# Projections with extra columns instead of carries, a GpSimd copy at the end of a solve, and a state written in place (hybrid mLSTM / RWKV-7 block, one core)

## The chip, the cores and the metric

One Trainium2 chip, one of its cores. The metric is the device time of one execution in microseconds. Engines by the profile's names: PE is TensorE (PEld its weight loads), DVE is VectorE, ACT is ScalarE, POOL is GpSimd, SP is SyncE, whose queue issues all DMAs of this kernel.

## The reference, cut to what matters

One layer on 2048 tokens of width 1024: a mixer with two groups of heads (mLSTM and RWKV-7), then cross-attention, a SwiGLU FFN and a final norm. The change lies in the mixer alone. What of it matters here:

```
z = u @ w_in                                # both groups
# RWKV-7: every projected channel is mixed with the one of the token before
z = z + (token_shift(z) - z) * mu           # r, k, v, and the three low-rank inputs
# mLSTM: a causal convolution over 4 tokens, then silu
out = zp[:, 0:T] * w[0] ... + zp[:, 3:3 + T] * w[3]     # zp: 3 zeros ahead
# RWKV-7 recurrence, a 64 x 64 state S per head
sa = einsum('bhij,bhj->bhi', S, a_t)
S = S * w_t + sa * b_t + v_t * k_t ;  y_t = S r_t
```

## The kernel before, in words

Everything is computed with channels on partitions and tokens in columns. The normed input `u` lies in DRAM as two float16 parts (`u_d[0]` high, `u_d[1]` low); a product of full accuracy is three float16 matmuls (`mm3`, lines 53 to 55).

`mixer_pass` runs twice (`hq` 0 and 1), each time over half of the heads. A pass walks over 8 groups (`sg`) of 256 tokens. For each group it does:

- `load_u` (line 624): 8 DMAs bring the 256 columns of `u`.
- `prepare` for two blocks of 128 channels (`e` 0 and 1): `project` gives k, r and v of RWKV-7 in PSUM (24 matmuls of 256 columns each). `shifted` (lines 284 to 290) mixes neighbouring tokens: ACT writes `ps * mu` into columns 1 to 256 of a tile `tmu` (line 287), POOL puts the last column of the group before into column 0 (line 286) and saves the last one (line 288), and DVE adds `ps * (1 - mu)` to the shifted tile (line 289). The rest of `prepare` builds the operands of the chunk form: chunks of 64 tokens, a triangular 64 x 64 matrix `MX` per head and chunk, values `VS`, `VX`, keys `KBt`.
- `solve` (lines 400 to 452) inverts the triangular matrices. Four DMAs turn 32 x 32 blocks of `MX` through DRAM into a tile `M`, one block per partition; POOL does 31 steps of two instructions each (lines 424, 426), a chain in which each waits for the one before; ACT copies the result `X` turned into `M` (line 427, 512 elements, read with a step). Then 12 DMAs on SP: `X` to `t1d` (line 430) and `M` to `td` (line 429) in DRAM, and back as `T1` (line 434) and into `MX` (line 439). PE joins the blocks with `pps` (line 444), which waits for `T1`, and `xps` (line 450), which waits for `MX`; ACT copies each result.
- `scan` (lines 454 to 493): four chunks one after the other. First ACT copies the state `st.S` into the chunk operand `VS` (line 457). Each chunk is 16 small matmuls into `ch` with two ACT copies between (lines 464, 469), then DVE adds the old state (line 475) and multiplies by the decay into `VS` of the next chunk (line 478), or, after the fourth chunk, into a tile `Sc` (line 481).
- `mlstm` for two heads: `project` for q and k (`qps`), ACT writes the scaled product into a tile `z` at columns 3 to 258 (line 543), POOL brings and saves the three columns of the group before (lines 542, 544), ACT starts the convolution with the last tap (line 547), DVE adds three taps (line 549). `vops` (line 558, by `mm3`) gives values and gate, with `u` as the weights.

The loop is written group after group, and the order on each engine is set when the kernel is built, by the framework's own estimate of when each instruction can start. Instructions of one group are so laid between those of others: the mLSTM projections of one group fill PE while POOL solves. At run time each engine goes through its list in order; an instruction that waits holds up all behind it. PSUM tiles for projections (`mm`) and for small products (`ax`) have two buffers each.

Of the kernel before, what the change touches and what calls it, by code (L numbers as in the profile page):

```python
# [7 lines left out]
F32 = mybir.dt.float32  # L8
# [235 lines left out]
def mixer_pass(c, I, hq, tp, T):  # L244

    nc, tc = c.nc, c.tc
    SGN = 256
    w_in = I["w_in"][0]
    b0, b1 = slice(0, 64), slice(64, 128)
# [13 lines left out]

    carry = tp.k.tile([P, 2, 3], F32, tag="carry", name="carry")
    nc.gpsimd.memset(carry, 0.0)
    halo = tp.k.tile([P, 2, 2, 3], F32, tag="halo", name="halo")
    nc.gpsimd.memset(halo, 0.0)
    st = Ctx()
    st.S = tp.k.tile([P, 2, 64], F32, tag="Sc", name="Sc", bufs=3)
    nc.gpsimd.memset(st.S, 0.0)  # L270
    st.Cn = []
# [3 lines left out]

    def project(ps, j, e, u):
        for k in range(KT):
            h, l = wts[j > 2][k]
            o = (2 * (j - 3 if j > 2 else j) + e) * P
            s = slice(o, o + P)  # L280
            mm3(nc, ps, (h[:, s], l[:, s]), u[k], k == 0, k == KT - 1)

    def shifted(ps, j, e, o):
        t = tp.t2.tile([P, SGN + 1], F32, tag="tmu", name="tmu")
        m = 4 * j + 2 * hq + e
        nc.gpsimd.tensor_copy(t[:, 0:1], carry[:, e, j:j + 1])
        nc.scalar.activation(t[:, 1:SGN + 1], ps, AF.Copy, scale=c.mu_s[:, m:m + 1])
        nc.gpsimd.tensor_copy(carry[:, e, j:j + 1], t[:, SGN:SGN + 1])
        nc.vector.scalar_tensor_tensor(o, ps, c.mu_c[:, m:m + 1], t[:, 0:SGN], op0=ALU.mult, op1=ALU.add)
        return o  # L290

    def group(sg):
        G = Ctx()
        G.xwa = [tp.t2.tile([P, SGN], F16, tag=f"xwa{i}", name="xwa") for i in range(2)]
        for i in range(2):
            nc.sync.dma_start(G.xwa[i], c.l_d[0][i][:, sg * SGN:(sg + 1) * SGN])
        G.MX = tp.MX.tile([P, 2, 4, 64], F32, tag="MX", name="MX")
        G.VS = tp.sg.tile([P, 2, 4, 2, 64], F32, tag="VS", name="VS")
        G.VX = tp.sg.tile([P, 2, 4, 2, 64], F32, tag="VX", name="VX")
        G.bon = tp.sg.tile([P, 2, SGN], F32, tag="bon", name="bon")  # L300
        G.W = tp.sg.tile([P, 2, 4, 1], F32, tag="W", name="W")
        return G

    def prepare(sg, e, u, G):
# [31 lines left out]

        ps = tp.pmm.tile([P, SGN], F32, tag="mm", name="kps")
        project(ps, 1, e, u)
        k = shifted(ps, 1, e, tp.t2.tile([P, SGN], F32, tag="k", name="k"))
        ps = tp.pmm.tile([P, SGN], F32, tag="mm", name="rps")  # L340
        project(ps, 0, e, u)
        r = shifted(ps, 0, e, tp.t2.tile([P, SGN], F32, tag="r", name="r"))
        ps = tp.pmm.tile([P, SGN], F32, tag="mm", name="vps")
        project(ps, 2, e, u)
# [55 lines left out]
    def solve(MX, NG):  # L400
# [18 lines left out]
        for s in range(31):  # L419
# [6 lines left out]
            nc.gpsimd.tensor_tensor(X[:, s + 1:32, 0:ncl], X[:, s + 1:32, 0:ncl], tv, ALU.add)  # L426
        nc.scalar.copy(M[:, 0:16], X.rearrange("p r c -> p c r"))
        for e in range(2):
# [25 lines left out]
    def scan(sg, gs, G):  # L454
        y = tp.s2.tile([P, 2, 2, 2, 64], F32, tag="y", name="y")
        for h in range(2):
            nc.scalar.copy(G.VS[halves[h], :, 0, h], st.S[halves[h]])
        for n in range(4):
            ch = tp.psc.tile([P, 2, 3, 64], F32, tag="ch", name="ch")
            for e, g in enumerate(gs):  # L460
                for h in range(2):
                    nc.tensor.matmul(ch[halves[h], e, 0], lhsT=g.RR[:, n, h, 0:64], rhs=G.VS[:, e, n, h], start=True, stop=True)
            R = tp.s2.tile([P, 2, 64], F32, tag="R", name="R")
            nc.scalar.copy(R, ch[:, :, 0])
            for e, g in enumerate(gs):
                for b in halves:
                    nc.tensor.matmul(ch[b, e, 1], lhsT=g.M[b, n], rhs=R[b, e], start=True, stop=True)
            for h, b in enumerate(halves):
                nc.scalar.copy(G.VX[b, :, n, h], ch[b, :, 1])
            for e, g in enumerate(gs):  # L470
                for h in range(2):
                    last = nc.tensor.matmul(ch[halves[h], e, 2], lhsT=g.KBt[:, n, h], rhs=G.VX[:, e, n, h], start=True, stop=True)
            Sn = tp.s2.tile([P, 2, 64], F32, tag="Sn", name="Sn")
            for h, b in enumerate(halves):
                nc.vector.tensor_tensor(Sn[b], ch[b, :, 2], G.VS[b, :, n, h], ALU.add)
            if n < 3:
                for h, b in enumerate(halves):
                    nc.vector.tensor_tensor(G.VS[b, :, n + 1, h], Sn[b], G.W[b, :, n].to_broadcast([64, 2, 64]), ALU.mult)
            else:
                st.S = tp.k.tile([P, 2, 64], F32, tag="Sc", bufs=3, name="Sc")  # L480
                nc.vector.tensor_tensor(st.S, Sn, G.W[:, :, n].to_broadcast([P, 2, 64]), ALU.mult)
        yps = tp.psc.tile([P, 2, 2, 2, 64], F32, tag="Y", name="yps")
# [46 lines left out]
    def mlstm(sg, e, u):  # L529
# [8 lines left out]
        for j in range(2):  # L538
            ps = tp.pmm.tile([P, SGN], F32, tag="mm", name="qps")
            project(ps, 3 + j, e, u)  # L540
            z = m2.tile([P, SGN + 3], F32, tag="z", name="z", bufs=1)
            nc.gpsimd.tensor_copy(z[:, 0:3], halo[:, e, j])
            nc.scalar.activation(z[:, 3:SGN + 3], ps, AF.Copy, scale=DSC)
            nc.gpsimd.tensor_copy(halo[:, e, j], z[:, SGN:SGN + 3])
            a = m2.tile([P, SGN], F32, tag="cv", name="cv", bufs=1)
            cw = lambda i: col(c, R_CONV + 8 * i + 4 * j + hp)
            nc.scalar.activation(a, ps, AF.Copy, scale=c.cw3[:, 4 * j + hp:4 * j + hp + 1])  # L547
            for i in range(3):
# [10 lines left out]
        for n in range(2):  # L559
            ts = slice(n * P, (n + 1) * P)  # L560
            for k in range(KT):
                h, l = wts[1][k]
                mm3(nc, ps[:, n], (u[k][0][:, ts], u[k][1][:, ts]),
                    [x.rearrange("p (j e d) -> p j e d", j=4, e=2)[:, 2:4, e] for x in (h, l)], k == 0, k == KT - 1)
# [53 lines left out]
    def load_u(sg):  # L618
        u = []
        for k2 in range(KT // 2):  # L620
            h = tp.u.tile([P, 2, SGN], F16, tag="uh", name="uh")
            l = tp.u.tile([P, 2, SGN], F16, tag="ul", name="ul")
            for i, t in enumerate((h, l)):
                nc.sync.dma_start(t, c.u_d[i][:, 2 * k2:2 * k2 + 2, sg * SGN:(sg + 1) * SGN])
            u += [(h[:, 0], l[:, 0]), (h[:, 1], l[:, 1])]
        return u
# [8 lines left out]

    NS = T // SGN
    late = []
# [784 lines left out]
```

## Time and profile before

| | |
|---|---|
| median of 3 runs | 3060.55 us (3058.68 to 3062.34) |
| the profiled execution | 3062.21 us |
| its span, first to last instruction | 3060.5 us |
| busy in the span: PE | 2922.1 us (95%) |
| DVE, ACT, POOL | 2034.8, 1262.3, 1180.1 us |
| mean granted TensorE clock | 0.981 of 2.4 GHz |

The mixer passes lie between about 100 and 1260 us of the span; before them is the pass that norms the input, behind them output projection, attention and FFN. Busy time of PE counts each matmul to its modelled end, so a PE that is 95% busy may have little or no time to give. "Idle before" is the time in which an engine had nothing running, and the name behind the arrow is what ended it. A granted clock of 1.00 is the upper of TensorE's two levels, 0.50 the lower; a number between is a stretch that had both.

### The profile page before, as it was taken

The page shows a single profiled execution, that of the slowest core. Times are in us where ns is not written, and L with a number is a line of the kernel's source. Part 1 is how long each engine was busy: PE and PEld are TensorE (multiplying, and loading weights), DVE is VectorE, ACT ScalarE, POOL GpSimd, SP SyncE. Part 2 cuts the span into 40 slices and gives each one's busy share as a digit, 9 for nine tenths or more (in the row PEclk, how much of TensorE's full clock was granted, in tenths as well). Part 3 has the DMA queues.
Part 4 walks back from the last instruction along what each step waited for, and adds up shares of the span by engine and source line. Part 5 has one row for each costly group of instructions (what it writes and reads, how often), then busy time and mean ns, then how long its engine had stood idle before and what let it go on. Part 6 is the DMA issues. An engine that isn't in the chain of part 4 may idle for free. (4 is left out here: it accounts for less than half of the span.)

```text
span 3060.5 us, 54611 instructions
## 1 busy us (share of the span) xinstructions
PE 2922.1 (95%) x20579; PEld 1772.5 (58%) x20579; DVE 2034.8 (66%) x3652; ACT 1262.3 (41%) x2842; POOL 1180.1 (39%) x2149
## 2 busy tenths in 40 slices
PE   7899999999999988999999999999999999899998
PEld 4677877778777767665455544444444444344443
DVE  6666666777666666565588886545445555988975
ACT  6544444555444445454456653222222223423432
POOL 2164655555456654032111144222222222644542
PEclk9999999999999988999999999999999999999999
DMA  8621112232211213554223366111111121554442
GB/s 278 143 60 44 45 43 47 78 99 55 53 50 44 56 45 111 183 186 145 97 93 125 110 227 201 57 55 56 56 55 58 57 62 63 185 184 143 159 137 76
DMA packets 330212, 307.85 MB, mean 101 GB/s; under 512 B 88302, under 2 KB 280028, under 8 KB 329052
## 3 DMA queue, kind: packets, MB, share of 16 engines
q1 hardware_dynamic: 329948, 304.36, 32.3%
q8 instruction: 162, 2.65, 0.4%
q14 instruction: 102, 0.84, 0.1%
HBM read 208.79 MB, written 95.49 MB: 99 GB/s over the span
## 5 line engine op out<-in xcount | busy, mean ns | idle before, releaser
L53 PE MATMUL pp<-u,wb 128*128 128x512 f16 x1232 | 467.9, 380 | 14.0 <-DVE e L1127 9.6
L54 PE MATMUL pp<-u,wb 128*128 128x512 f16 x1232 | 467.9, 380 | 0.0
L55 PE MATMUL pp<-u,wb 128*128 128x512 f16 x1232 | 467.6, 380 | 0.0
L1127 DVE TENSOR_TENSOR e<-pp,e 128x512 f32<-128x512 f32 x308 | 208.5, 689 | 302.0 <-PE pp L55 289.1
L55 PE MATMUL dps<-w,gS 128*128 128x512 f16 x616 | 233.4, 379 | 9.0 <-DVE gS L49 9.0
L54 PE MATMUL dps<-w,gS 128*128 128x512 f16 x616 | 233.5, 379 | 1.7 <-DVE w L49 1.7
L53 PE MATMUL dps<-w,gS 128*128 128x512 f16 x616 | 233.5, 379 | 0.0
L424 POOL TENSOR_TENSOR tmp<-M,X 64x126 f32<-64x126 f32 (+22 forms) x496 | 189.1, 381 | 98.8 <-DMA M<-md 71.4
L426 POOL TENSOR_TENSOR X<-X,tmp 64x126 f32<-64x126 f32 (+22 forms) x496 | 202.2, 408 | 29.0
L54 PEld LDWEIGHTS <-wb 128*128 128x128 f16 x1232 | 120.7, 98 | 156.5 <-issue 12.9
L53 PEld LDWEIGHTS <-wb 128*128 128x128 f16 x1232 | 120.8, 98 | 151.0 <-DMA u<-u_d 5.4
L55 PEld LDWEIGHTS <-wb 128*128 128x128 f16 x1232 | 120.7, 98 | 146.3 <-issue 1.1
L1143 POOL TENSOR_TENSOR S<-raw 128x512 f32<-128x512 f32 x22 | 33.3, 1513 | 413.4 <-DVE wb L49 413.4
L53 PE MATMUL qps<-uh,wh 128*128 128x256 f16 x512 | 143.8, 281 | 9.5 <-ACT cv L547 9.5
L53 PE MATMUL vops<-wh,uh 128*128 128x256 f16 x512 | 143.2, 280 | 3.1 <-ACT cv L547 3.1
L54 PEld LDWEIGHTS <-wh 128*128 128x128 f16 x1280 | 127.1, 99 | 31.3 <-issue 11.6
L54 PE MATMUL qps<-ul,wh 128*128 128x256 f16 x512 | 143.7, 281 | 0.0
L55 PE MATMUL qps<-uh,wl 128*128 128x256 f16 x512 | 143.5, 280 | 0.0
L55 PE MATMUL vops<-wh,ul 128*128 128x256 f16 x512 | 143.0, 279 | 0.0
L54 PE MATMUL vops<-wl,uh 128*128 128x256 f16 x512 | 142.9, 279 | 0.0
L53 PEld LDWEIGHTS <-wh 128*128 128x128 f16 x1280 | 127.1, 99 | 24.5 <-issue 2.7
L55 PEld LDWEIGHTS <-wl 128*128 128x128 f16 x1280 | 127.2, 99 | 20.6 <-issue 1.9
(423 smaller groups left out, 7637.6 us busy)
## 6 DMA issues: line engine op xcount, KB each, us to landing
g_d<-e SPq DMA_DIRECT2D x88, 256.0 KB
h<-h_d SPq DMA_DIRECT2D x32, 512.0 KB
acc<-h_d SPq DMA_DIRECT2D x32, 512.0 KB
u_d<-ub SPq DMA_DIRECT2D x56, 256.0 KB
ga<-g_d SPq DMA_DIRECT2D x32, 384.0 KB
raw<-in_ffn_w_gate_dram SPq DMA_DIRECT2D x22, 512.0 KB
raw<-in_ffn_w_up_dram SPq DMA_DIRECT2D x22, 512.0 KB
rawd<-in_ffn_w_down_dram SPq DMA_DIRECT2D x22, 512.0 KB
```

The lines of the kernel that those rows point to most:

```text
L53: nc.tensor.matmul(out, lhsT=lhs[0], rhs=rhs[0], start=start, stop=False)
L54: nc.tensor.matmul(out, lhsT=lhs[0], rhs=rhs[1], start=False, stop=False)
L55: nc.tensor.matmul(out, lhsT=lhs[1], rhs=rhs[0], start=False, stop=stop)
L424: nc.gpsimd.tensor_tensor(tv, M[:, s, s + 1:32].unsqueeze(2).to_broadcast(shp), X[:, s, 0:ncl].unsqueeze(1).to_broadcast(shp), ALU.mult)
L426: nc.gpsimd.tensor_tensor(X[:, s + 1:32, 0:ncl], X[:, s + 1:32, 0:ncl], tv, ALU.add)
L1127: add = lambda o, x, y: nc.vector.tensor_tensor(o, x, y, ALU.add)
L1143: nc.gpsimd.tensor_tensor(s[0], a[1][0], a[1][1], ALU.add)
```

## The change

- No carries: `load_u` brings 260 columns, 4 of the group before and 256 of its own (for the first group POOL writes zeros into the 4). `project` computes 257 columns for k, r and v and 259 for q and k of mLSTM, so the preceding tokens are computed again. `shifted` reads the same PSUM tile at two offsets; `z` is written whole by ACT. All `carry`, `halo` and `tmu` tiles and their 320 POOL copies go.
- The last copy of a solve (`M` from `X`) is done by POOL instead of ACT.
- The state after the fourth chunk is written by DVE in two halves straight into `VS` of the next group; the `Sc` tile, its product and the two ACT copies at the start of each scan go. After the last group of a pass no state is computed.

The diff, cut to its core:

```diff
     def project(ps, j, e, u):
...
-            mm3(nc, ps, (h[:, s], l[:, s]), u[k], k == 0, k == KT - 1)
+            mm3(nc, ps, (h[:, s], l[:, s]), [x[:, SGN + 4 - ps.shape[1]:SGN + 4] for x in u[k]], k == 0, k == KT - 1)
     def shifted(ps, j, e, o):
-        t = tp.t2.tile([P, SGN + 1], F32, tag="tmu", name="tmu")
         m = 4 * j + 2 * hq + e
-        nc.gpsimd.tensor_copy(t[:, 0:1], carry[:, e, j:j + 1])
-        nc.scalar.activation(t[:, 1:SGN + 1], ps, AF.Copy, scale=c.mu_s[:, m:m + 1])
-        nc.gpsimd.tensor_copy(carry[:, e, j:j + 1], t[:, SGN:SGN + 1])
-        nc.vector.scalar_tensor_tensor(o, ps, c.mu_c[:, m:m + 1], t[:, 0:SGN], op0=ALU.mult, op1=ALU.add)
+        nc.scalar.activation(o, ps[:, 1:SGN + 1], AF.Copy, scale=c.mu_c[:, m:m + 1])
+        nc.vector.scalar_tensor_tensor(o, ps[:, 0:SGN], c.mu_s[:, m:m + 1], o, op0=ALU.mult, op1=ALU.add)
         return o
+    def values():
+        return tp.sg.tile([P, 2, 4, 2, 64], F32, tag="VS", name="VS")
     def group(sg):
         G = Ctx()
+        G.VS = st.VS
+        if sg == 0:
+            G.VS = values()
+            for h in range(2):
+                nc.gpsimd.memset(G.VS[halves[h], :, 0, h], 0.0)
...
-        nc.scalar.copy(M[:, 0:16], X.rearrange("p r c -> p c r"))
+        nc.gpsimd.tensor_copy(M[:, 0:16], X.rearrange("p r c -> p c r"))
...
     def scan(sg, gs, G):
-        for h in range(2):
-            nc.scalar.copy(G.VS[halves[h], :, 0, h], st.S[halves[h]])
+        st.VS = values() if sg < NS - 1 else None
...
+            dst = G.VS[:, :, n + 1] if n < 3 else st.VS[:, :, 0] if st.VS is not None else None
+            if dst is None:
+                break
             Sn = tp.s2.tile([P, 2, 64], F32, tag="Sn", name="Sn")
             for h, b in enumerate(halves):
                 nc.vector.tensor_tensor(Sn[b], ch[b, :, 2], G.VS[b, :, n, h], ALU.add)
-            if n < 3:
-                for h, b in enumerate(halves):
-                    nc.vector.tensor_tensor(G.VS[b, :, n + 1, h], Sn[b], G.W[b, :, n].to_broadcast([64, 2, 64]), ALU.mult)
-            else:
-                st.S = tp.k.tile([P, 2, 64], F32, tag="Sc", bufs=3, name="Sc")
-                nc.vector.tensor_tensor(st.S, Sn, G.W[:, :, n].to_broadcast([P, 2, 64]), ALU.mult)
+            for h, b in enumerate(halves):
+                nc.vector.tensor_tensor(dst[b, :, h], Sn[b], G.W[b, :, n].to_broadcast([64, 2, 64]), ALU.mult)
...
-            nc.gpsimd.tensor_copy(z[:, 0:3], halo[:, e, j])
-            nc.scalar.activation(z[:, 3:SGN + 3], ps, AF.Copy, scale=DSC)
-            nc.gpsimd.tensor_copy(halo[:, e, j], z[:, SGN:SGN + 3])
+            nc.scalar.activation(z, ps, AF.Copy, scale=DSC)
...
-            h = tp.u.tile([P, 2, SGN], F16, tag="uh", name="uh")
+            h = tp.u.tile([P, 2, SGN + 4], F16, tag="uh", name="uh")
...
+                o = 0
+                if sg == 0:
+                    nc.gpsimd.memset(t[:, :, 0:4], 0.0)
+                    o = 4
+                nc.sync.dma_start(t[:, :, o:], c.u_d[i][:, 2 * k2:2 * k2 + 2, sg * SGN - 4 + o:(sg + 1) * SGN])
```

Since the build decides the order anew, the change also moves instructions within the mixer; from the first matmuls of the attention on, all engines have the same order as before. Two places:

SP at the end of the sixth solve of the first pass, before (`T_...` is `T1`):

```order
L430 DMA t1d<-X 16x512 x2
L429 DMA td<-M 512x1x32 x2
L434 DMA T_7497<-t1d 32x8x16 x4
L439 DMA MX<-td 32x8x32 x4
L296 DMA xwa<-l_d_88 128x256
```

The same place with the change:

```order
L431 DMA t1d<-X 16x512 x2
L435 DMA T_7343<-t1d 32x8x16 x2
L430 DMA td<-M 512x1x32 x2
L435 DMA T_7343<-t1d 32x8x16 x2
L298 DMA xwa<-l_d_88 128x256
L440 DMA MX<-td 32x8x32 x4
```

The first two loads of `T1`, which wait for `t1d` to land, have moved ahead of the two stores of `M`; 14 of the 16 solves have it so, one has one load ahead, one has the old order.

ACT around the end of the same solve, before:

```order
L543 ACTIVATE z<-qps 128x256
L547 ACTIVATE cv<-qps,cw_499 128x256
L397 COPY KBt<-kbps 128x4x64
L551 ACTIVATE th<-cv 128x256
L427 COPY M<-X 64x512
L397 COPY KBt<-kbps 128x4x64
L543 ACTIVATE z<-qps 128x256
L547 ACTIVATE cv<-qps,cw_499 128x256
```

The same place with the change:

```order
L541 ACTIVATE z<-qps 128x259
L544 ACTIVATE cv<-qps,cw_499 128x256
L548 ACTIVATE th<-cv 128x256
L541 ACTIVATE z<-qps 128x259
L398 COPY KBt<-kbps 128x4x64
L544 ACTIVATE cv<-qps,cw_499 128x256
L398 COPY KBt<-kbps 128x4x64
L548 ACTIVATE th<-cv 128x256
```

The copy of `M` is gone from between the two copies of `KBt` that empty PSUM for PE; the rest stands in much the same order.

## Rows read from the trace of the kernel before

**Rows 1.** The page: busy us over the span, share, instructions.

```profile
PE 2922.1 (95%) x20579; PEld 1772.5 (58%) x20579; DVE 2034.8 (66%) x3652; ACT 1262.3 (41%) x2842; POOL 1180.1 (39%) x2149
```

**Rows 2.** Busy time by stretch: the mixer, and all behind it. Columns: start and end, length, then busy us (instructions) of PE, PEld, DVE, ACT, POOL, granted clock, DMA share, GB/s.

```profile
130.00:1200.00 1070.00, 1011.56 (x10555) 820.67 (x10552) 716.66 (x1714) 505.22 (x1431) 592.59 (x1595) 0.96 0.24 56
1262.00:3060.00 1798.00, 1755.00 (x8515) 839.03 (x8513) 1192.16 (x1665) 637.37 (x1168) 554.60 (x450) 1.00 0.34 114
```

**Rows 3.** The longest waits of PE between 180 and 1180 us: us in total, times, longest.

```profile
PE pps L444 <- DMA T<-t1d: 10.3, 12, 1.8
PE kbps L395 <- ACT KBt L397: 6.8, 7, 2.6
PE qps L53 <- ACT cv L547: 5.4, 8, 1.8
```

**Rows 4.** The timeline of PE, nine of its stops (seven behind an ACT copy, two for `T1`): start, length, instruction, and in brackets the idle time before it and what ended it.

```profile
254.96 0.81 PE L444 MATMUL pps<-T,MX 32*32 32x32 f32 x30 [1.81 <-DMA T<-t1d]
...
394.21 0.46 PE L395 MATMUL kbps<-ident,KB 64*128 64x64 f32 x4 [1.69 <-ACT KBt L397]
...
463.66 0.37 PE L53 MATMUL vops<-wh,uh 128*128 128x256 f16 x1 [2.16 <-ACT cv L547]
...
530.59 0.48 PE L321 MATMUL wps<-xwa,lwa 64*128 64x256 f16 x3 [1.46 <-ACT KBt L397]
...
600.35 0.69 PE L395 MATMUL kbps<-ident,KB 64*128 64x64 f32 x4 [2.58 <-ACT KBt L397]
...
602.02 0.79 PE L321 MATMUL wps<-xwa,lwa 64*128 64x256 f16 x3 [0.98 <-ACT KBt L397]
...
745.10 0.21 PE L444 MATMUL pps<-T,MX 32*32 32x32 f32 x2 [1.26 <-DMA T<-t1d]
...
796.77 0.33 PE L462 MATMUL ch<-VS,RR 128*64 128x64 f32 x2 [2.52 <-ACT VS L457]
...
1075.17 1.22 PE L350 MATMUL sps<-sq,bones 128*128 128x256 f32 x2 [4.09 <-ACT sq L348]
```

**Rows 5.** Busy time in the stretches of the seven ACT stops, columns as in rows 2.

```profile
392.00:402.00 10.00, 8.31 (x77) 5.95 (x76) 5.01 (x12) 5.29 (x15) 4.56 (x10) 0.83 0.32 54
460.00:470.00 10.00, 7.81 (x54) 5.36 (x53) 5.90 (x14) 5.20 (x14) 5.50 (x13) 0.83 0.28 45
528.00:538.00 10.00, 8.39 (x65) 5.64 (x65) 5.81 (x13) 4.92 (x14) 5.01 (x11) 0.83 0.31 54
598.00:610.00 12.00, 8.67 (x77) 5.87 (x78) 8.10 (x17) 7.27 (x19) 5.27 (x9) 0.72 0.42 91
795.00:805.00 10.00, 8.23 (x71) 6.17 (x72) 5.10 (x10) 6.21 (x16) 6.23 (x11) 0.66 0.27 42
1071.00:1095.00 24.00, 16.37 (x158) 11.63 (x157) 11.87 (x26) 9.99 (x25) 5.74 (x14) 0.57 0.19 40
```

**Rows 6.** The timeline of ACT ahead of the third stop, and all its waits for the end of a solve between 180 and 1180 us.

```profile
529.22 1.05 ACT L427 COPY M<-X 64x512 f32<-64x512 f32 x1 [1.31 <-POOL X L426]
530.17 0.36 ACT L397 COPY KBt<-kbps 128x256 f32<-128x256 f32 x1
...
ACT M L427 <- POOL X L426: 24.3, 15, 3.6
```

**Rows 7.** The timeline of PE in a run of projections at the upper clock: the second and the ninth matmul of a row of equal ones.

```profile
613.46 0.27 PE L54 MATMUL qps<-ul,wh 128*128 128x256 f16 x1
...
614.23 0.27 PE L55 MATMUL qps<-uh,wl 128*128 128x256 f16 x1
```

**Rows 8.** The timeline of SP's issues and of POOL at the end of the sixth solve (the last step of the solve ended at 529.18).

```profile
529.21 0.78 SPq L430 DMA_DIRECT2D t1d<-X  x2
530.29 1.23 SPq L429 DMA_DIRECT2D td<-M  x2
531.62 2.09 SPq L434 DMA_DIRECT2D T<-t1d  x4
534.03 1.78 SPq L439 DMA_DIRECT2D MX<-td  x4
...
531.37 0.52 POOL L414 MEMSET X<- 64x512 f32 x1 [2.05 <-DMA t1d<-X]
```

**Rows 9.** The small POOL copies (duration min/median/max in ns, then first and last start) and two waits between 180 and 1180 us, as in rows 3.

```profile
L542 POOL COPY z<-halo x64: 176/186/696, 104.0 to 1180.4; 128x3 f32<-128x3 f32 x64
...
ACT tmu L287 <- POOL carry L288: 27.8, 15, 3.6
POOL tmp L424 <- DMA M<-md: 65.0, 15, 8.0
```

**Rows 10.** Two POOL instructions by line, between 180 and 1262 us: count, busy us, mean ns, idle before.

```profile
L503 POOL TENSOR_TENSOR y<-y,var 128x512 f32<-128x512 f32 x15 | 15.6, 1042 | 0.1
L377 POOL COPY VX<-VS 64x256 f32<-64x256 f32 x60 | 25.2, 419 | 23.3 <-ACT VS L375 19.8 <-POOL z L542 0.9
```

**Rows 11.** Two more stops of PE, as in rows 4, and the product that makes the next chunk's state, by line, as in rows 10.

```profile
850.55 0.76 PE L462 MATMUL ch<-VS,RR 128*64 128x64 f32 x8 [0.62 <-ACT VS L457]
1185.48 0.33 PE L462 MATMUL ch<-VS,RR 128*64 128x64 f32 x2 [0.59 <-ACT VS L457]
...
L478 DVE TENSOR_TENSOR VS<-Sn,W 64x128 f32<-64x128 f32 x96 | 31.0, 322 | 2.0
```

**Rows 12.** Float32 matmuls of the mLSTM chunks over the whole span, as in rows 9; the moving operand of every second one starts 129 elements into its tile.

```profile
L585 PE MATMUL ncp<-vx,Em x128: 275/276/582, 152.4 to 1194.5; 128*128 128x129 f32 x128
```

More of the change, by code (lines that the diff above doesn't have):

```diff
@@ L247, in mixer_pass @@
     SGN = 256
+    NS = T // SGN
     w_in = I["w_in"][0]
@@ L262, in mixer_pass @@
             wts[n - 3].append((h, l))
[L264 to L267, printed above, removed]
     st = Ctx()
-    st.S = tp.k.tile([P, 2, 64], F32, tag="Sc", name="Sc", bufs=3)
-    nc.gpsimd.memset(st.S, 0.0)
+    st.VS = None
     st.Cn = []
@@ L297, in group @@
         G.MX = tp.MX.tile([P, 2, 4, 64], F32, tag="MX", name="MX")
-        G.VS = tp.sg.tile([P, 2, 4, 2, 64], F32, tag="VS", name="VS")
         G.VX = tp.sg.tile([P, 2, 4, 2, 64], F32, tag="VX", name="VX")
@@ L335, in prepare @@
         nc.gpsimd.tensor_copy(G.W[:, e], E[:, :, 64:65])
-        ps = tp.pmm.tile([P, SGN], F32, tag="mm", name="kps")
+        ps = tp.pmm.tile([P, SGN + 1], F32, tag="mm", name="kps")
         project(ps, 1, e, u)
         k = shifted(ps, 1, e, tp.t2.tile([P, SGN], F32, tag="k", name="k"))
-        ps = tp.pmm.tile([P, SGN], F32, tag="mm", name="rps")
+        ps = tp.pmm.tile([P, SGN + 1], F32, tag="mm", name="rps")
         project(ps, 0, e, u)
         r = shifted(ps, 0, e, tp.t2.tile([P, SGN], F32, tag="r", name="r"))
-        ps = tp.pmm.tile([P, SGN], F32, tag="mm", name="vps")
+        ps = tp.pmm.tile([P, SGN + 1], F32, tag="mm", name="vps")
         project(ps, 2, e, u)
@@ L538, in mlstm @@
         for j in range(2):
-            ps = tp.pmm.tile([P, SGN], F32, tag="mm", name="qps")
+            ps = tp.pmm.tile([P, SGN + 3], F32, tag="mm", name="qps")
             project(ps, 3 + j, e, u)
             z = m2.tile([P, SGN + 3], F32, tag="z", name="z", bufs=1)
-            nc.gpsimd.tensor_copy(z[:, 0:3], halo[:, e, j])
-            nc.scalar.activation(z[:, 3:SGN + 3], ps, AF.Copy, scale=DSC)
-            nc.gpsimd.tensor_copy(halo[:, e, j], z[:, SGN:SGN + 3])
+            nc.scalar.activation(z, ps, AF.Copy, scale=DSC)
             a = m2.tile([P, SGN], F32, tag="cv", name="cv", bufs=1)
             cw = lambda i: col(c, R_CONV + 8 * i + 4 * j + hp)
-            nc.scalar.activation(a, ps, AF.Copy, scale=c.cw3[:, 4 * j + hp:4 * j + hp + 1])
+            nc.scalar.activation(a, ps[:, 3:SGN + 3], AF.Copy, scale=c.cw3[:, 4 * j + hp:4 * j + hp + 1])
             for i in range(3):
@@ L559, in mlstm @@
         for n in range(2):
-            ts = slice(n * P, (n + 1) * P)
+            ts = slice(n * P + 4, (n + 1) * P + 4)
             for k in range(KT):
@@ L620, in load_u @@
         for k2 in range(KT // 2):
-            h = tp.u.tile([P, 2, SGN], F16, tag="uh", name="uh")
-            l = tp.u.tile([P, 2, SGN], F16, tag="ul", name="ul")
+            h = tp.u.tile([P, 2, SGN + 4], F16, tag="uh", name="uh")
+            l = tp.u.tile([P, 2, SGN + 4], F16, tag="ul", name="ul")
             for i, t in enumerate((h, l)):
-                nc.sync.dma_start(t, c.u_d[i][:, 2 * k2:2 * k2 + 2, sg * SGN:(sg + 1) * SGN])
+                o = 0
[3 more added lines that the diff above has]
+                nc.sync.dma_start(t[:, :, o:], c.u_d[i][:, 2 * k2:2 * k2 + 2, sg * SGN - 4 + o:(sg + 1) * SGN])
             u += [(h[:, 0], l[:, 0]), (h[:, 1], l[:, 1])]
@@ L634, in run_mlstm @@
                 mtails.pop(0)()
-    NS = T // SGN
     late = []
```

## The prediction

> **What bounds the kernel now.** I read the page's busy times first, then the busy time by stretch, then PE's waits, its timeline, and the timeline of the engine that PE waits for. PE is busy for 2922 of 3060 us [rows 1]. Behind the mixer it is busy for 1755 of 1798 us at a granted clock of 1.00 [rows 2], and there all engines keep their order, so I expect nothing from that part. In the mixer two things are to be seen: PE stands for 1070 - 1011.6 = 58 us, and its clock is 0.96 on average [rows 2], about 0.04 x 1012 = 40 us of work at the upper level lost. So some 100 us are there to be had, and the change can only win them by ending PE's stops, or lose by adding work to PE or new stops. PE's longest waits are for `T1`, for `KBt` and for the convolution's tile, the last two on ACT [rows 3].
>
> The clock falls where PE stood: in six stretches, each with a stop of 1.5 to 4.1 us [rows 4], the granted clock is 0.57 to 0.83 [rows 5]. A stop therefore costs its length and some slow matmuls behind it.
>
> **The change, part by part.**
>
> *Extra columns.* Seven equal matmuls of 256 columns take 614.23 - 613.46 = 0.77 us [rows 7], 0.110 us each, 0.43 ns per column. k, r and v are 2 passes x 8 groups x 2 blocks x 3 x 24 = 2304 matmuls with one column more, q and k of mLSTM 2 x 8 x 2 x 2 x 24 = 1536 with three more: 6912 columns, **+3.0 us**, on the path, since PE is the bound.
>
> *ACT's copy of the solved blocks leaves ACT.* This is the largest term. At 529.22 ACT had waited 1.31 us for POOL's last step of the solve, then copied for 1.05 us; only then came the `KBt` copy, at 530.17 [rows 6], and PE, which waited for that, went on at 530.59 after 1.46 us [rows 4]. With the wait and the copy gone, `KBt` could come 2.36 us earlier, more than the stop. Seven stops of rows 4 lie within some 3 us of such a copy, at six solves of sixteen. They sum to 15.5 us. In their stretches the lost clock is busy time x (1 - clock) [rows 5]: 1.4 + 1.3 + 1.4 + 2.4 + 2.8 + 7.0 = 16.4 us. Upper end of the gain: 32 us. What ACT gets back at a solve is on average 24.3 / 15 + 1.05 = 2.7 us [rows 6], as long as the stops of one solve, 15.5 / 6 = 2.6. Lower end: nothing, for the next latecomer is near. PE's waits for `T1` come at other solves than these stops, as at 254.96 and 745.10 [rows 4]; where a stop of ACT came first, PE reached `pps` late enough. So at these six solves PE would now meet `T1`, 10.3 / 12 = 0.9 us a time on average and 1.8 at most [rows 3]: of 2.6 us some 0.9 to 1.8 turn into another wait, and the order is remade besides. I take half, between what is left by the one (two thirds) and by the other (a third): **-16 us**.
>
> *The same copy on POOL.* Bounds for its duration: twice the 0.42 us of a copy of half the elements, 0.84, and the 1.04 us of a product of the same size with two inputs [rows 10], or more, since it reads with a step; I take 0.9. Behind it on POOL is the clearing of the next `X`, which stood for 2.05 us anyway until `t1d` had landed [rows 8], and then the next solve, whose first step waited 65 us in all for its matrices [rows 9]: hidden. `td` is behind it on SP, where the new order puts the first two loads of `T1` ahead; those wait for `t1d`, landed at about 531.4, 2.2 us after the solve's end, and take half of 2.09 us to issue [rows 8]. So `td` cannot go before 3.3 us, and the copy has that long. The Trainium skill's page "GPSIMD Engine Reference", section "3. Performance versus the Vector engine", speaks against the move: GpSimd takes about twice as long as VectorE for ordinary elementwise work, though section "4.1 Engine selection" counts instructions with one input, as a copy is, near the full rate. By the first, set on ACT's row, the copy would be an estimated 2.1 us: the sum would stay, and the return trip below would have some 0.02 more of a chance, with 1.2 us of cover left instead of 2.4. No row of this trace has the copy on POOL.
>
> *SP's order.* Second pair of `T1` loads: before, all four were issued by 533.71; now 531.4 + 1.05 + 1.23 (`td`) + 1.05 = 534.7, **1.0 us later**. `td` ends at 533.6 instead of 531.5, so `MX` may come up to 2.1 us later [rows 8]. Behind these loads on SP are other prefetches; PE waits at `pps` and `xps`. Upper end: the 12 waits for `T1` [rows 3] each 1.0 us longer, and as much again in clock (16.4 to 15.5, as above): 25 us. Lower end: -10, all of them gone, since PE's list is laid anew around the later loads. I take **+3**, near zero: both the loads and the work that fills PE are moved together.
>
> *The state.* The two ACT copies at a scan's start go; two stops that ended with them, 0.62 and 0.59 us, are not among those above [rows 11]: **-1.2**. DVE gets one product of 0.32 us more per group [rows 11] and loses the last state of each pass; it is busy 67% of the mixer [rows 2]: 0.
>
> *The carries.* 320 POOL copies of about 0.19 us go [rows 9], 60 us of POOL's time, which bounds nothing. ACT waited 27.8 us for the carry [rows 9], but none of PE's longest waits ends there [rows 3], so these are hidden: 0. In their place ACT now waits until the readers of the last k, r or v are done, since it writes these tiles itself; DVE had that wait before. Stops too short to stand among the longest, at most 0.3 us at each of the 15 waits, bound both sides: +-4.5.
>
> *Loads of 260 columns and 16 clearings of 4 columns*: the DMA share in the mixer is 0.24 [rows 2], and the clearings stand on POOL ahead of a wait for `M` [rows 9]: 0.
>
> Sum: 3.0 - 16 + 3 - 1.2 = **-11.2 us**. The sum is made against the profiled execution, 3062.2 us (span 3060.5): 3051.0. That execution is 1.7 us above the median of the runs shown, so **3049 us**.
>
> **The rivals.**
>
> - *More comes back.* All of the 32 us return and SP's order costs nothing: 3062.2 + 3.0 - 32 - 1.2 - 1.7 = 3030. For it: ACT's freed time is as long as the stops. Against it: an order made anew has misfits of its own.
> - *The stops move on.* ACT is free, but PE meets the next latecomer (`T1`, the convolution) at nearly the same time; 5 us remain: 3062.2 + 3.0 - 5 - 1.2 + 3 - 1.7 = 3060. For it: the waits for `T1` that stand at the other solves [rows 3, 4]. Against it: those are shorter, 1.8 us at most, where ACT's stops reach 2.6 and 4.1 [rows 4].
> - *Slower: the solve's return trip.* The mechanism is the `T1` pair ahead of `td` on SP; its place is every solve's end; its price is the 25 us above, and the ACT part shrinks to 10, since PE then waits at `pps` instead: 3062.2 + 3.0 + 25 - 10 - 1.2 - 1.7 = 3077. It decides where 7 or more solves are so exposed: the gain without SP's term is 16 + 1.2 - 3.0 = 14.2, and 7 x 1.0 x 2.06 = 14.4. Against it: PE's list has been moved with the loads.
> - *The odd start.* The moving operands now begin 3 or 1 float16 elements into a row. Float32 operands that begin 129 elements in take what the others take, 275 to 276 ns [rows 12]; an odd half-word is nowhere in the trace. Were such a matmul to take twice as long, 3840 x 0.110 = 422 us would come on top: 3468.
>
> **How the numbers follow.** Forecast 0.47, more back 0.15, stops move on 0.23, return trip 0.13, odd start 0.02. A measurement of this kernel tells about 0.2%, 6 us, from no change, so faster begins below 3054. The forecast's own range is 3040 to 3056, so 0.44 of it and the 0.15 make faster 0.59; the third case and the forecast's edge, 0.03, less 0.01 at that case's own upper edge, make the same 0.25; the rest is 0.16. The range, 3028 to 3065, takes in the forecast, more back, and the stops that move on with the carries' bound of 4.5; it leaves out the two slower cases.
>
> **What would show it.** Right: the 16 copies of `M` on POOL at 0.8 to 1.1 us and no wait of ACT for the end of a solve; PE's idle time between 130 and the mixer's end down from 58 to some 50 us and its clock up from 0.96 to about 0.97; matmuls of 257 and 259 columns within 2 ns of the old ones; the stretch behind the mixer as long as before, about 1798 us. Wrong: waits of PE for `T1` and `MX` of more than 25 us (the return trip); new stops behind ACT's writes of k, r and v or behind DVE's state (another wait in place of the old); stops in equal number and length at other places (the stops move on); a projection cadence above 0.115 us (the odd start).

## The result, and the profile after

The changed kernel takes 3090.8 us (3086.8 to 3092.9, 4 runs), the one before 3059.6 beside it: ratio 1.010, interval 1.0082 to 1.0117, **some 31 us slower**. The forecast was 3049, its range ended at 3065: the prediction was wrong, in sign too.

The profile of after, first the page's busy times (as [rows 1]):

```profile
PE 2932.9 (95%) x20579; PEld 1777.4 (58%) x20579; DVE 2047.4 (66%) x3660; ACT 1238.3 (40%) x2794; POOL 1152.0 (37%) x1859
```

Then the stretches: from 130 us to the first matmul of the output projection (`ops`), and from there to the end; columns as in [rows 2]. Before, cut at the same matmul:

```profile
130.00:1265.56 1135.56, 1069.67 (x11179) 869.16 (x11177) 759.99 (x1817) 546.88 (x1535) 596.73 (x1600) 0.96 0.25 63
1265.56:3060.50 1794.94, 1752.50 (x8494) 837.15 (x8493) 1191.46 (x1664) 635.69 (x1166) 552.36 (x448) 1.00 0.34 114
```

After:

```profile
130.00:1289.78 1159.78, 1073.00 (x11110) 869.10 (x11110) 772.69 (x1829) 522.65 (x1486) 571.04 (x1317) 0.96 0.25 62
1289.78:3088.30 1798.52, 1757.98 (x8570) 840.62 (x8569) 1193.00 (x1667) 636.64 (x1169) 554.03 (x450) 1.00 0.34 114
```

24 of the 28 us between the two profiles lie ahead of `ops`. PE's clock there is the same, its busy time grew by 3.3 us, and it stands for 1159.8 - 1073.0 = 87 us instead of 66. The cut is not quite the same in both: in after, 76 matmuls of the mixer's last group stand behind the first `ops` (x8570 against x8494). Over the whole span busy time grew by 10.8 us, from 2922.1 to 2932.9, and the time that PE stands by 17. What ended PE's stops in that stretch of after (columns as in [rows 3]):

```profile
PE pps L445 <- DMA T<-t1d: 28.4, 17, 3.4
PE qps L53 <- ACT cv L544: 6.6, 8, 3.6
PE trps L799 <- DVE xn L810: 5.7, 2, 5.0
PE ymps L607 <- DVE yt L604: 5.7, 2, 3.0
PE ch L462 <- DVE VS L480: 4.6, 3, 3.2
PE kbps L396 <- ACT KBt L398: 4.6, 8, 1.2
```

Summed over all rows of that view, by what ended the stop: before, ACT 42.3, `T1` 16.1, DVE 4.4 us; after, ACT 26.0, `T1` 28.4, DVE 27.5. So **ACT's stops fell by 16 us, and 35 us of others came.** (The forecast's -16 is another 16: about half of it was stops and half slow clock behind them.) Against the nine of [rows 4] stand such stops of after:

```profile
209.25 0.24 PE L445 MATMUL pps<-T,MX 32*32 32x32 f32 x2 [3.41 <-DMA T<-t1d]
...
761.50 0.22 PE L445 MATMUL pps<-T,MX 32*32 32x32 f32 x2 [3.08 <-DMA T<-t1d]
...
1096.68 0.31 PE L445 MATMUL pps<-T,MX 32*32 32x32 f32 x2 [3.15 <-DMA T<-t1d]
...
1211.01 0.69 PE L462 MATMUL ch<-VS,RR 128*64 128x64 f32 x6 [3.24 <-DVE VS L480]
...
1231.61 1.94 PE L799 MATMUL trps<-ident,xn 128*128 128x128 f32 x8 [5.00 <-DVE xn L810]
```

SP and POOL at the end of the sixth solve (the last step ended at 535.45), as [rows 8], and POOL's copy by line:

```profile
535.48 0.78 SPq L431 DMA_DIRECT2D t1d<-X  x2
537.06 0.81 SPq L435 DMA_DIRECT2D T<-t1d  x2
537.97 1.23 SPq L430 DMA_DIRECT2D td<-M  x2
539.30 1.06 SPq L435 DMA_DIRECT2D T<-t1d  x2
540.41 0.45 SPq L298 DMA_DIRECT2D xwa<-l_d  x1
540.96 3.18 SPq L440 DMA_DIRECT2D MX<-td  x4
...
535.52 1.06 POOL L428 COPY M<-X 64x512 f32<-64x512 f32 x1
...
L428 POOL COPY M<-X 64x512 f32<-64x512 f32 x16 | 17.8, 1115 | 1.0
```

From the solve's end, `T1` is issued by 4.9 us instead of 4.5, `td` by 3.8 instead of 2.3, `MX` by 8.7 instead of 6.6 [rows 8]. The copy on POOL hides, as predicted. `ACT M <- POOL X` [rows 6] and `ACT tmu <- POOL carry` [rows 9] are gone; `ACT k L282 <- DVE sq`, 24.3 us, is new. The stops of [rows 11] for the state now end with DVE's `VS`, 4.6 us in all. The longest, 3.24 us at 1211.01, shows what a list can do: between the two halves of the state's product the build put an instruction that waits for POOL, and the second half, which needs nothing from it, came 3 us late:

```profile
1207.03 0.28 DVE L480 TENSOR_TENSOR VS<-Sn,W 64x128 f32<-64x128 f32 x1
1210.26 0.37 DVE L601 SCALAR_TENSOR_TENSOR r<-r,ss 128x2 f32<-128x2 f32 x1 [2.94 <-POOL ss L600]
1210.66 0.29 DVE L480 TENSOR_TENSOR VS<-Sn,W 64x128 f32<-64x128 f32 x1
```

### The profile page after: what moved, and what is told of

Read it like the earlier page. It is cut to its first block, busy times and chain, and to the rows that moved or that the text cites. A ratio compares the mean times of both kernels' runs of the same rounds, so it can differ in the third digit from the quotient of the medians.

```text
span 3088.3 us, 54027 instructions
## 1 busy us (share of the span) xinstructions
PE 2932.9 (95%) x20579; PEld 1777.4 (58%) x20579; DVE 2047.4 (66%) x3660; ACT 1238.3 (40%) x2794; POOL 1152.0 (37%) x1859
## 5 line engine op out<-in xcount | busy, mean ns | idle before, releaser
L53 PE MATMUL pp<-u,wb 128*128 128x512 f16 x1232 | 467.9, 380 | 14.6 <-DVE e L1127 10.1
L427 POOL TENSOR_TENSOR X<-X,tmp 64x126 f32<-64x126 f32 (+22 forms) x496 | 211.3, 426 | 35.7
L53 PE MATMUL qps<-uh,wh 128*128 128x259 f16 x512 | 147.7, 289 | 7.8 <-ACT cv L544 6.6
L55 PE MATMUL qps<-uh,wl 128*128 128x259 f16 x512 | 146.9, 287 | 0.0
L54 PE MATMUL qps<-ul,wh 128*128 128x259 f16 x512 | 146.8, 287 | 0.0
```

Of the source, the lines that this page charges most:

```text
L53: nc.tensor.matmul(out, lhsT=lhs[0], rhs=rhs[0], start=start, stop=False)
L54: nc.tensor.matmul(out, lhsT=lhs[0], rhs=rhs[1], start=False, stop=False)
L55: nc.tensor.matmul(out, lhsT=lhs[1], rhs=rhs[0], start=False, stop=stop)
```

## The experiments

In all tables, us against before is the ratio less one, times 3060, with its interval; stops are PE's from 130 us to the first `ops`, by what ended them, summed as above.

### One part at a time, the order made anew by each build

**e1**, the change, the copy back on ACT:

```diff
-        nc.gpsimd.tensor_copy(M[:, 0:16], X.rearrange("p r c -> p c r"))
+        nc.scalar.copy(M[:, 0:16], X.rearrange("p r c -> p c r"))
```

> The changed kernel, with one line undone: ACT copies M again, and POOL does not. In the order that is built, SP issues td ahead of all T1 loads at 15 of 16 solves, as in the kernel before. Theory 1 (the return trip: the copy on POOL makes the build put T1 ahead of td on SP, and this makes T1 and MX late): nearly all of the 31 us goes, 3055 to 3068 us, PE's wait for T1 back from 28 to 8 to 14 us. Rival 2 (extra columns and the missing carries cost it): 3080 us or more, T1 wait small but another one in its place. Rival 3 (any order made anew lies somewhere within 20 us of the other): anything from 3045 to 3095, with no tie to SP's order.

**e2**, the kernel before with the reverse edit:

```diff
-        nc.scalar.copy(M[:, 0:16], X.rearrange("p r c -> p c r"))
+        nc.gpsimd.tensor_copy(M[:, 0:16], X.rearrange("p r c -> p c r"))
```

> The kernel before, with one line changed: POOL copies M instead of ACT. SP issues at least one T1 load ahead of td at 15 of 16 solves. Theory 1 (return trip): as slow as the whole change, 3082 to 3095 us, T1 wait 22 to 35 us. Rival 2 (columns and carries): 3045 to 3062 us, since ACT is freed and nothing else is changed. Rival 3 (order luck): anything from 3045 to 3095.

**e3**, the change with `T1` behind `td` on SP (`last` is the second store of `M`); **e6**, the same on e2:

```diff
+                with tc.issue_after(last.ins):
-                nc.sync.dma_start(T1[...], t1d[e, h]...)
+                    nc.sync.dma_start(T1[...], t1d[e, h]...)
```

> The changed kernel, copy on POOL kept, but the T1 loads are tied behind the last store of M (td) on SP, as all of the kernel before had them. Theory 1 (return trip): the T1 wait falls below 14 us and the gain that was predicted for ACT comes through in part, 3045 to 3065 us. Rival 4 (PE comes to pps earlier because ACT's stops are gone, and waits for T1 in any order of SP): T1 wait stays over 22 us and the time at 3080 to 3095 us. Rival 3 (order luck): anything from 3045 to 3095.

> The kernel before with the copy on POOL, and the T1 loads tied behind td on SP. If SP's order costs what it seemed to in the changed kernel (3091 with it, 3075 with the loads tied behind): PE's wait for T1 down from 21 to 12 to 16 us, ACT's stops at 27 us as with the POOL copy alone, 3045 to 3056 us. Rival (the order on SP is worth nothing on this base, another wait takes its place): 3057 to 3065 us, as with the POOL copy alone (3062).

**e4**, the kernel before with the parts of the diff on `project`, `shifted`, `z` and `load_u` alone; **e8**, with those on `VS` and `Sc` alone:

```diff
# e4
-            mm3(nc, ps, (h[:, s], l[:, s]), u[k], k == 0, k == KT - 1)
+            mm3(nc, ps, (h[:, s], l[:, s]), [x[:, SGN + 4 - ps.shape[1]:SGN + 4] for x in u[k]], ...)
# e8
-            nc.scalar.copy(G.VS[halves[h], :, 0, h], st.S[halves[h]])
+        st.VS = values() if sg < NS - 1 else None
```

> The kernel before with only the first part of the change: extra columns, no carries, no halos; ACT copies M, the state goes by Sc as before. SP has td ahead of T1 at 15 of 16 solves. Theory 1 (return trip): 3 us of columns and nothing else, 3055 to 3070 us. Rival 2 (columns and carries cost it): 3080 to 3095 us. Rival 3 (order luck): anything from 3045 to 3095.

> The kernel before with only the state part: DVE writes the state in two halves straight into VS of the next group, no copies by ACT at a scan's start. If the state is worth what the prediction took (1.2 us less): 3053 to 3060 us. Rival (the two DVE products and PE's new wait for DVE at the first ch of a group cost more than ACT's copies did; the kernel with both parts reached the output projection 7 us after the one with no carries alone): 3062 to 3070 us.

**e5**, the kernel before with SP's order of the change:

```diff
+            last = nc.sync.dma_start(T1[0:32, :, 16 * e:16 * e + 16], t1d[e, 0]...)    # both e
+        with tc.issue_after(last.ins):
+            ...                                                                        # td, both e
```

> The kernel before, ACT copies M, but on SP the first two loads of T1 are tied ahead of the two stores of M (td), as the changed kernel has it: SP's order alone. Return trip: T1 complete some 0.4 us and MX 0.7 to 1.0 us later at every solve, PE's wait for T1 before the output projection up from 16 to 22 to 28 us, 3064 to 3075 us. Rival (SP's order costs nothing by itself; the loss comes from PE, ACT and DVE meeting otherwise): T1 wait within 4 us of before, 3054 to 3062 us.

**e7**, e4 with even starts and widths:

```diff
-        ps = tp.pmm.tile([P, SGN + 1], F32, tag="mm", name="kps")    # r, v too
+        ps = tp.pmm.tile([P, SGN + 2], F32, tag="mm", name="kps")
-            ps = tp.pmm.tile([P, SGN + 3], F32, tag="mm", name="qps")
+            ps = tp.pmm.tile([P, SGN + 4], F32, tag="mm", name="qps")
```

> The kernel with the no-carries part alone, but each projection computes one column more: 258 from the third column of a row for k, r and v, 260 from the first for q and k, so every moving operand begins at an even float16 element. In the run with 257 and 259 columns the cadence was 111.2 and 112.0 ns against 109.4 for 256, 1.3 ns more than the columns ask for (0.43 ns each). If the odd start or the odd width costs these 1.3 ns: 110.3 and 111.1 ns now, 3.4 us less than the no-carries part alone, 3062 to 3068 us. Rival (any width above 256 costs about 1.3 ns a matmul): 111.6 and 112.4 ns, 3067 to 3073 us.

| order made anew | median | us against before | `T1` | ACT | DVE |
|---|---|---|---|---|---|
| before | 3057 to 3061 | | 16.1 | 42.3 | 4.4 |
| the change | 3090.8 | +31 (25 to 36) | 28.4 | 26.0 | 27.5 |
| e1 change, copy on ACT | 3070.3 | +11 (7 to 16) | 20.6 | 44.7 | 12.2 |
| e2 POOL's copy alone | 3062.4 | +3 (0 to 6) | 21.4 | 27.0 | 18.2 |
| e3 change, `td` first | 3075.0 | +15 (11 to 19) | 18.9 | 26.7 | 27.0 |
| e4 no carries alone | 3068.7 | +11 (6 to 16) | 12.2 | 38.6 | 14.5 |
| e5 SP's order alone | 3071.8 | +11 (7 to 15) | 14.6 | 37.2 | 20.6 |
| e6 POOL's copy, `td` first | 3064.0 | +4 (1 to 6) | 14.5 | 36.1 | 16.1 |
| e7 no carries, even | 3056.7 | -3 (-6 to -1) | 9.5 | 36.6 | 13.0 |
| e8 state alone | 3071.3 | +10 (6 to 14) | 12.0 | 41.4 | 18.8 |

The return trip (theory 1: the loads of `T1` ahead of `td` make `T1` and `MX` late), my first theory, does not stand as the whole: e2 has it at 15 of 16 solves and loses 3 us, not 31; e5 loses 11, but its wait for `T1` did not grow. e1 and e3 take 20 and 16 us off, and both should then have come near 3060. What all rows share is the last column: **every kernel whose order was made anew stands 12 to 28 us for DVE, the kernel before 4.** Parts as unlike as the columns, the state and SP's order alone each cost 10 to 11 us. This speaks for the third theory, that the order itself costs. The column is no measure of the loss, though: e2 and e7 stand 18 and 13 us for DVE and come out at +3 and -3.

Several expectations missed. e1, e2 and e8 came out just above the nearest narrow range that was named, e3 between two of them, and e7 5 us below both of its own, with cadences (the time from one matmul of a row to the next) of 110.7 and 111.3 ns, between the two that were expected. In e6 the wait for `T1` fell as the first account had it, but the time was the rival's.

### The order held fixed

To hold it, each engine's list of instructions was read from the built kernel before, matched with the new kernel's, and every instruction from the mixer on tied behind its old predecessor in issue order, with no wait added:

```diff
+        for a, b in zip(order, order[1:]):
+            tc.add_manual_dep(own[b], own[a].name, mybir.DependencyInfo(mybir.DependencyClass.NoSync, mybir.DependencyReason.DATA))
```

PE has the same matmuls in all kernels, so its list carries over whole. ACT's 96 writes of k, r and v are left free where they go straight into their tiles: in their old places they would wait for readers that stand behind them. Pinned were: e9 the change, e13 the change with even columns, e14 the part of e4, e15 that of e8, e12 that of e2, all engines; e10 the edit of e5, all but the solve's transfers on SP; e16 the change on PE and SP, e17 on PE alone. e11 is the kernel before, unedited, in the order of e5 but with `td` first. No run ties the unedited kernel to its own order; e15, nearly the same work, shows no change.

> The changed kernel, whole, but with the mixer's order on PE, DVE, POOL, SP and ACT pinned to that of the kernel before, wherever an instruction of the one has its like in the other (ACT's writes of k, r and v, DVE's state products and POOL's copy of M are left to the build). SP has td ahead of T1 as before. If the loss is the re-made order and not the work (theory 3): 3045 to 3064 us, PE's stops for DVE back from 27 to under 12 us. If the work itself costs it (columns, state, POOL's copy): 3075 us or more, with the stops still there.

> The kernel before, every engine pinned to its own old order, but for the transfers at the solve's end on SP: the first two loads of T1 ahead of td. Nothing else moves, so this is the price of SP's order by itself. Return trip (theory 1): 3067 us or more, PE's wait for T1 and MX up by 8 us or more. Theory 3 (order made anew is what cost in e5_t_first, 3072): 3057 to 3066 us.

> The kernel before, work unchanged and td ahead of T1 on SP, but PE, DVE, ACT, POOL and the rest of SP pinned to the order that the build made for e5_t_first (3072 us). Theory 3 (the order alone): 3066 to 3076 us, with PE's stops for DVE near the 20 us of e5_t_first. Return trip (theory 1): 3056 to 3064 us, since T1 and MX come as early as before.

> The kernel before, every engine pinned to its old order, ACT's copy of M gone, POOL's put where the build puts it (after the solve's last step); td ahead of T1 as before. The prediction's largest term by itself: -16 us gives 3044; ACT's stops would fall from 42 to some 27 us. Theory 3 expects part of it, 3044 to 3056 us. Rival (the stops move on to the next latecomer whatever the order): 3056 to 3064 us.

> e9_change_old_order (the whole change in the old order, 3053 us) with one column more per projection, so that each begins at an even float16 element (258 and 260 columns). Cadence by e7: 110.6 and 111.2 ns against 111.2 and 112.0, some 2.6 us less: 3048 to 3053 us. Rival (the 12 us between e4 with odd and e7 with even columns came from the columns and not from the order made anew): 3038 to 3044 us.

> The kernel before with the no-carries part alone (257 and 259 columns), in the old order; ACT's writes of k, r and v and POOL's first clearings are left to the build. If nothing but the columns counts, at the cadence measured in e4 (1.75 ns more for 2304 matmuls, 2.6 for 1536): 8 us more, 3064 to 3071 us. If the missing carries give time back (e9 lies 6 us below before in spite of the columns): 3053 to 3062 us. If the part costs more than the columns by itself, as e4 seemed to show: 3071 us or more.

> The kernel before with the state part alone, in the old order. The prediction took 1.2 us less: 3054 to 3061 us. If the work itself costs the 10 us of e8: 3066 us or more.

> The whole change with only PE and SP pinned to the old order; DVE, ACT and POOL as the build then lays them. If it is the place of PE's work that costs in the order made anew: 3050 to 3060 us, as with all engines pinned (3053). If it is DVE's and ACT's order: 3068 us or more, with PE's stops for DVE at 20 us or more.

> The whole change with PE alone pinned to the old order; SP is left to the build, which puts T1 ahead of td again at 15 of 16 solves. If PE's order is the cause and SP's costs what it cost in the old order (6.5 us, e10): 3055 to 3065 us. If SP's order is the larger part of the loss: 3070 us or more, PE's wait for T1 at 24 us or more.

| order pinned | median | us against before | `T1` | ACT | DVE |
|---|---|---|---|---|---|
| e9 the change | 3053.2 | -7 (-9 to -4) | 14.0 | 30.5 | 6.9 |
| e10 SP's order alone | 3065.9 | +7 (4 to 9) | 21.5 | 42.2 | 7.7 |
| e11 before's work, order of e5 | 3075.8 | +16 (12 to 20) | 17.6 | 36.8 | 22.0 |
| e12 POOL's copy alone | 3051.7 | -9 (-12 to -6) | 21.5 | 29.9 | 7.3 |
| e13 change, even columns | 3046.1 | -12 (-16 to -8) | 14.3 | 29.7 | 6.6 |
| e14 no carries alone | 3055.7 | -4 (-7 to -2) | 12.1 | 34.7 | 8.1 |
| e15 state alone | 3061.3 | 0 (-2 to +3) | 19.4 | 41.2 | 6.9 |
| e16 change, PE and SP | 3054.8 | -6 (-8 to -3) | 13.4 | 28.6 | 13.3 |
| e17 change, PE alone | 3064.3 | +6 (3 to 10) | 20.9 | 27.6 | 14.0 |

The same work that takes 3091 us as built takes 3053 in the old order, and the old work takes 3076 in another order. In e9 PE's waits in the mixer and its stretch read:

```profile
PE pps L445 <- DMA T<-t1d: 14.0, 12, 3.9
PE qps L53 <- ACT cv L544: 8.3, 10, 3.3
PE ch L472 <- ACT VX L469: 4.0, 2, 3.4
PE kbps L396 <- ACT KBt L398: 3.3, 7, 0.7
...
130.00:1256.57 1126.57, 1073.96 (x11213) 869.73 (x11210) 772.16 (x1834) 526.87 (x1491) 563.83 (x1319) 0.97 0.26 64
```

PE's busy time over the whole span is near after's (2928.7 to 2932.9); the stretch is 33.2 us shorter, and so, by 32 us, are the stops: 52 us instead of 84. The 14 us of `T1` and the 21 of DVE are gone, most of ACT's gain stays. In e11 DVE's stops are back, spread over many tiles:

```profile
PE trps L799 <- DVE ss L602: 3.7, 1, 3.7
PE vps L53 <- DVE k L289: 3.1, 1, 3.1
...
PE trps L799 <- DVE xn L810: 2.5, 1, 2.5
```

e9, e11, e12, e16 and e17 fell into the ranges of the account by order, e14 into that of carries which give time back. e10 stands at its upper edge (3065.9 of 3066), e15 0.3 us above its own. e13 lies between its two ranges: 4.6 us below e9, each against its own before, where the cadences give 2.5; the rest is within the noise.

**Which engine's order.** With PE's list alone pinned the change stands at +6, with SP's as well at -6, with all at -7, with none at +31. So 24 us came back with PE's list, and 12 more when SP had `td` first; by the intervals, give or take some 6 and 4. But the lists that were left free did not stay as they were in after: the build laid them anew around the pinned ones. Compared instruction by instruction in the traces, the mixer's list of DVE in e16 has 94% of e9's order and 74% of after's. So the 24 us belong to PE's list with what follows from it on the other engines, and e16 does not show that DVE's, ACT's and POOL's lists of after cost nothing. e3 cannot tell SP's share either: its list of PE differs from after's (91% in common) nearly as much as e9's does (89%).

SP's order has no one price: 12 us within the change (e17 against e16), 7 on the kernel before (e10), and nothing that the noise leaves to be seen where the rest was in the order of e5: with the loads first +11 (e5), with `td` first +16 (e11). e2 and e6, where the rest was laid anew, are at +3 and +4.

**What each part is worth in the old order, and what its re-made order took:** no carries -4 instead of +11, the state 0 instead of +10, POOL's copy with `td` first -9 instead of +4, SP's order +7 instead of +11. The order that the build made took 10 to 15 us from each of the first three edits, 38 from all together; the 4 of SP's order are within the noise.

**e18**, cadences alone: four kinds of projection in one program, in the order that its build made.

```diff
+        at = (2, 1, 2, 1, 1)[j]
-            mm3(nc, ps, (h[:, s], l[:, s]), [x[:, SGN + 4 - ps.shape[1]:SGN + 4] for x in u[k]], k == 0, k == KT - 1)
+            mm3(nc, ps, (h[:, s], l[:, s]), [x[:, at:at + ps.shape[1]] for x in u[k]], k == 0, k == KT - 1)
```

> The kernel of e4 with four kinds of projection in one program: k 258 columns from an odd element, r 257 from an even one, v 258 from an even one, q and k of mLSTM 259 from an odd one as before. (k, r and v so mix tokens that lie one or two earlier; only the cadences are read.) If the odd start costs the extra 1.2 ns: k at some 111.7, r at 110.0, v at 110.6, q at 112.0 ns. If the odd number of columns costs it: k at 110.6, r at 111.2, v at 110.6, q at 112.0.

Neither expectation holds whole: k (258, odd start) 111.4, r (257, even start) 110.8, v (258, even) 110.7, q (259, odd) 111.9 ns. Odd starts cost 0.5 to 0.7 ns more than even ones of the same width. From an even start 257 columns take 1.3 ns more than 256, not 0.43. Whether the first column above 256 costs that is not shown: 256 columns were measured from element 0, 257 and 258 from element 1, 2 or 3. The 260 columns of e7, from element 0, take 1.9 more than 256, near their share of 1.7. So the start may be what costs, and no run separates the two.

## Why the prediction was wrong, step by step

- **The failed step is the one on the order.** The term for the copy said "the order is remade besides" and SP's term "I take +3, near zero: both the loads and the work that fills PE are moved together". Moving both was taken as a reason for no cost. It was most of the cost: the whole change is at +31 as built and at -7 in the old order, 38 us. For PE's list the sum had no term; holding it gave back 24 (e17, with the lists that the build then laid around it). SP's +3 stands against 12 within the change (e17 against e16) and 7 on the kernel before (e10); both lie under the upper end that was named, 25. The return-trip rival (3077) had the place and the wait: PE's wait for `T1` is 28.4 us, over its 25. But with that trip alone the change would stand near 3066 (e17).
- **ACT's copy, -16.** The stops that ended with ACT fell by 16.3 us in after and by 12.4 in e12, where nothing else moved. Of that e12 gained 9 us, since PE met `T1` in their place, as argued: those stops grew from 16.1 to 21.5, and DVE's from 4.4 to 7.3. The mechanism was right, its size nearly twice too large. The bound of 1.8 us for a wait for `T1` was read between 180 and 1180 us; behind that the kernel before has a longer one, at the last solve:

```profile
1204.22 0.28 PE L444 MATMUL pps<-T,MX 32*32 32x32 f32 x2 [4.30 <-DMA T<-t1d]
```

- **The copy on POOL, 0.9 us, hidden.** In after 13 of the 16 take 1.02 to 1.16 us and three up to 1.44; hidden, as argued. ACT took 1.05 [rows 6]. The Trainium skill's page "GPSIMD Engine Reference", section "4.1 Engine selection", has one-input work near the full rate; this row does not show it, since the copy, read with a step, takes as long as a product of the same size with two inputs, 1.04 [rows 10]. The estimate of 2.1 us, twice ACT's time, is not borne out: no copy took that long.
- **Extra columns, +3.0.** Mis-sized: 8. From 325.47 to 327.60, 19 steps of q (259 columns) in after take 112.1 ns each, where [rows 7] had 110:

```profile
325.47 0.27 PE L54 MATMUL qps<-ul,wh 128*128 128x259 f16 x1
...
327.60 0.28 PE L55 MATMUL qps<-uh,wl 128*128 128x259 f16 x1
```

  Over all unbroken rows of at least eight steps at the upper clock it is 109.4 to 109.5 ns for 256 columns, 111.3 for 257 and 112.0 for 259: 2304 x 1.8 + 1536 x 2.5 = 8.0 us. PE's busy time over the whole span agrees: 2929.7 us in e14 against 2922.1. The odd-start rival (twice as long) is out; an odd start costs 0.5 to 0.7 ns.
- **The carries, 0.** Worth some 12 us by difference, over the 4.5 that was named as a bound: e14 gains 4 in spite of 8 for the columns. The prediction dropped ACT's 27.8 us of waiting for POOL [rows 9] because none of PE's longest waits ends there. But an ACT that comes late to `tmu` is late for what stands behind it in its list too, and that shows under other names: in e14 PE's stops for ACT fell from 42.3 to 34.7 us, for `T1` from 16.1 to 12.1. That these are the same microseconds is argued, not shown. The new wait of ACT for the readers of k is there, 24.3 us in after, and 13.9 in e14, which gains all the same.
- **The state, -1.2.** e15: 0 (-2 to +3); the interval takes in the forecast.
- **Behind the mixer, nothing.** Right: 1798.5 against 1794.9 us in the two profiles, of which after's has the 76 matmuls of the mixer in it; the other profiles of the tables lie at 1791 to 1796.

Without SP's term the forecast for the work is 3.0 - 16 - 1.2 = -14 us. The parts measured in the old order give -4 + 0 - 9 = -13, the whole -7. That the first two agree is luck: the copy was taken 7 us too high, the columns 5 too low, and the 12 of the carries were left out. The order was not judged at all. e13, the change in the old order with even columns, is the fastest version measured: 3046.1 us, ratio 0.9962 (0.9949 to 0.9975) to before, some 42 us below the change as built.

Open: why the build lays PE's list so badly here. The runs show that the lists cost, not which estimate is off. Whether before's order is better than most is suggested (all re-made ones have more stops for DVE) but nine are few.

## What to carry to other kernels

Where a build makes the order anew, an edit's effect is its work plus a draw of the order, and at 95% busy the second can be the larger: here -7 and +38. Compare the lists first, price a moved list as a term of its own with a range, and before an edit is judged, run it once with the old order pinned on the bounding engine and on the queue that feeds it. A wait that an engine off the path loses may be worth microseconds under another name, so look at what stands behind it in its list.

## What was not expected of the hardware

In a row of equal float16 matmuls at the upper clock, one of 256 moving columns from element 0 takes 109.4 ns, 260 from element 0 111.3; from element 2, 257 take 110.8 and 258 110.7; from an odd element 257 take 111.3, 258 111.4, 259 112.0. So an odd start costs 0.5 to 0.7 ns, and 258 columns from an even element are cheaper than 257 from an odd one. GpSimd's copy of 512 float32 per partition, read with a step, takes 1.05 us in the median, as ScalarE's does (1.06).
